# Out-projection weights split beside the values' products, GLA in eight steps a half, and fewer stores of the last q and k

## The chip, the core and the metric

The kernel runs on one core of one Trainium2 chip. A core has five engines with a queue of instructions each: PE (TensorE, matrix products), DVE (VectorE), ACT (ScalarE), POOL (GpSimd) and SP (SyncE, which here issues nearly all transfers). Each works through its own queue in order; semaphores hold an instruction back until what it reads is there and what it overwrites has been read. The metric is the device time of one execution in microseconds (us), as the median of several runs.

## The reference

One layer of a decoder: 1024 tokens of width 1024, normed, go through one input projection; eight heads of differential attention and four heads of gated linear attention (GLA) run in parallel on its columns; the gated results are concatenated and go through one output projection of 2048 x 1024, a norm and the residual. Cut to what matters here:

```
h = rms_norm(x, pre_g)
z = h @ w_in                  # columns: qa ka va ga | qb kb vb gb | gk_low
# differential attention, 8 heads, two maps of 64, values of 128, causal
w  = softmax(q1 k1^T / 8) - lam * softmax(q2 k2^T / 8)
oa = rms_norm(w @ v, subln_g) * 0.8 * silu(ga)
# GLA, 4 heads, keys of 128, values of 256, in chunks of 64
S_t = diag(exp(log_a_t)) S_{t-1} + k_t^T v_t ;  o_t = q_t S_t
ob = rms_norm(o, gla_g) * silu(gb)
y  = concat(oa, ob) @ w_out
out = x + rms_norm(y, post_g)
```

All is float32.

## The kernel before

**Numbers in two parts.** A large product is taken as three products of rounded parts: each operand is split into `hi` (rounded on ACT) and `lo` (the rest, a subtraction on DVE), and hi x hi, lo x hi and hi x lo are summed in a bank of PSUM. So each operand costs a cast on ACT and a subtraction on DVE before PE can use it.

**Input projection.** `w_in` is taken in column blocks with a Strassen scheme: seven products instead of eight for a pair of 2 x 2 blocks. `order` (line 191 on) lists the steps. `("VB", n, kk)` and `("VA", n, kk)` are the wide steps of the GLA and attention values (24 matmuls of 512 columns each); `(p, n)` is product n of narrow pair p of `pairs` (12 matmuls). Each step's weights are split one to a few steps ahead (`prepare`, `block_weights`, `make_weights`). PE's product of n = 1, 6 and 7 goes to bank `x`, 2 and 4 to `y`, 5 and 3 to `z`. `take` and `take_values` finish a unit and store it to DRAM: `k_d`, `q_d` (attention keys and queries, `hi` and `lo`, four stores of 64 rows a unit), `v_d` (attention values), `gq_d`, `gv_d` and so on. Staging tiles of 2 KB a partition come from the tags `st` and `c`, four buffers each.

**Out-projection weights.** Each of the 32 pieces (128 rows x 512 columns, 256 KB) of `w_out` is loaded into `wo_raw` (tag `t4`, one buffer), split, and both parts stored to `wo_d` (`wo_step`, called by `go` behind each narrow step from pair 3 on: a load at n = 1 or 6, a split at n = 1 or 5). Later whole rows come back as `wo_hi`, `wo_lo` (`weights`).

**GLA** runs as a generator (`gla`), advanced by one step behind each narrow product from (8, 5) on, and what is left is run through where eight steps of `order` (`LEAD`) remain. For each head and each half of the tokens: transpose k (`pk`), products within chunks (`pa`), the norm of the half before (`gms`, `gla_norm`), states (`kv`, `gu`), results (two products `gpo`, copied by ACT to `go`), and the sum of squares split into `gqd`, which is the operand of the next `gms`. In `gla` each `yield` ends a step; a half has nine. `gla_norm` stores the finished results to `mixe`.

**Attention.** At the point of the last eight steps, `q`, `k`, `ks` of head 0 are loaded (`load_qk`; `ks` is k with its parts swapped), then weights 8 to 13, the first `mix` tile (token tile 0 of the GLA results, 1 MB in two parts) two steps later, weights 14 and 15. `merge` interleaves three streams by costs: scores (`sc`, minimum on DVE L1131, exponent on ACT L1141, scaling on POOL L1165 and subtraction on DVE L1169 to `p`), values (transposes `wtr`, split to `wt_hi`, `wt_lo`, products `po`) and the out-projection (`out_early`: `ypart`, the GLA half of each token tile as fill for PE, then the attention half, both kept in `y_d`). At the end partial results come back (`yp`) as seeds of the last products `yps`.

**Who sets the order.** The Python code lists instructions; a scheduler then orders each engine's queue by its own estimate of times. `keep_in_program_order` holds an engine's marked instructions in the order of the code (all matmuls, the last stores, the first mix and weight loads), and `issue_after` lets one instruction be issued only behind another. PE, DVE, ACT and SP all execute in the order fixed so.

## Time and profile before

| | |
|---|---|
| median of three runs | 1007.09 us (1006.35 to 1012.83) |
| profiled execution | 1006.61 us, span 1004.9 us |
| PE, DVE, ACT, POOL busy | 964.7, 737.9, 589.9, 144.0 us |
| granted clock of PE, mean | 0.993 |
| moved by DMA | 220.38 MB, mean 219 GB/s |

By the trace: the first scaled transposes of x start at 7.6 us; wide steps, with the first two products of pairs 0 to 2 between them, run until about 191 us; narrow pairs to 628, with GLA beside them from about 350; attention from 630 to about 960; the last products to 998. In stretches of 25 us:

| stretch (us) | PE busy | DVE busy | ACT busy | DMA share |
|---|---|---|---|---|
| 75 to 100 | 25.00 | 15.03 | 4.22 | 0.46 |
| 125 to 150 | 25.00 | 19.52 | 8.18 | 0.37 |
| 175 to 200 | 25.00 | 22.05 | 10.35 | 0.79 |
| 450 to 475 | 25.00 | 19.79 | 14.75 | 0.83 |
| 700 to 725 | 25.00 | 18.31 | 16.29 | 0.59 |

How to read the rows that follow: a row of waits is "engine line waited for: us in total, times, longest"; a row of time is start, duration, engine, line, operation, result<-operands, and in brackets the idle time of the engine before it and who ended it. In a row of a stretch stand its length, busy time with instructions of PE, PE's weight loads, DVE, ACT and POOL, then the granted clock, the DMA share and GB/s. `SPq` is an issue on SP's queue. A DMA row gives how many were issued, KB of each, and the median time from issue to landing.

### The profile page before, as it was taken

The page shows a single profiled execution, that of the slowest core. Times are in us where ns is not written, and L with a number is a line of the kernel's source. Part 1 is how long each engine was busy: PE and PEld are TensorE (multiplying, and loading weights), DVE is VectorE, ACT ScalarE, POOL GpSimd, SP SyncE. Part 2 cuts the span into 40 slices and gives each one's busy share as a digit, 9 for nine tenths or more (in the row PEclk, how much of TensorE's full clock was granted, in tenths as well). Part 3 has the DMA queues.
Part 4 walks back from the last instruction along what each step waited for, and adds up shares of the span by engine and source line. Part 5 has one row for each costly group of instructions (what it writes and reads, how often), then busy time and mean ns, then how long its engine had stood idle before and what let it go on. Part 6 is the DMA issues. An engine that isn't in the chain of part 4 may idle for free.

```text
span 1004.9 us, 14892 instructions
## 1 busy us (share of the span) xinstructions
PE 964.7 (96%) x4866; PEld 809.7 (81%) x4866; DVE 737.9 (73%) x1450; ACT 589.9 (59%) x1152; POOL 144.0 (14%) x153
## 2 busy tenths in 40 slices
PE   6999999999999999999999989799999999999887
PEld 4878888777888888888888877578888888888765
DVE  6996476888899768767787775567777677787545
ACT  8641232445476467755577764357666667777664
POOL 5410000000000000000000000112222233343232
PEclk9999999999999999999999999999999999999999
DMA  9544333755856867788968879896485499875467
GB/s 334 194 123 147 126 105 101 224 147 140 275 184 226 265 214 240 241 282 244 298 220 268 264 271 365 271 335 202 148 270 189 150 320 350 262 202 111 108 204 153
DMA packets 156845, 220.38 MB, mean 219 GB/s; under 512 B 16240, under 2 KB 83824, under 8 KB 156672
## 3 DMA queue, kind: packets, MB, share of 16 engines
q1 hardware_dynamic: 152736, 212.10, 65.4%
q0 software_dynamic: 4032, 7.34, 4.7%
q8 instruction: 38, 0.62, 0.2%
q14 instruction: 39, 0.32, 0.1%
HBM read 133.93 MB, written 88.60 MB: 221 GB/s over the span
## 4 chain that ended last, share of the span: by engine, by line
PE 73%; DMA 9%; DVE 8%; ACT 4%; issue 3%; SPq 1%; POOL 1%; DVEq 0%; ACTq 0%; POOLq 0%
PE x L117 13%; PE v L117 12%; PE ypart L117 11%; PE y L117 8%; PE z L117 8%; PE sc L117 6%; PE po L117 5%; PE yps L117 4%; PE wtr L120 2%; PE gpo L117 2%; DMA w_raw<-in_w_in_dram 2%; DMA k<-k_d 1%; PE kv L117 1%; DMA v_d<-v_hi 1%; DMA wo_d<-wo_raw 1%
## 5 line engine op out<-in xcount | busy, mean ns | idle before, releaser
L1141 ACT ACTIVATE p<-p,stt 128x896 f32<-128x896 f32 (+7 forms) x128 | 99.3, 777 | 47.5 <-DVE stt L1131 40.4
L329 DVE TENSOR_TENSOR w<-w_raw,w 128x512 fp32r<-128x512 f32 x134 | 91.7, 688 | 26.2 <-ACT w L327 26.1
L1131 DVE CUSTOM_DVE_ANT_0 p<-sc,maskt 128x512 f32<-128x512 f32 (+3 forms) x128 | 74.9, 586 | 46.5 <-PE sc L117 45.8
L327 ACT CAST w<-w_raw 128x512 fp32r<-128x512 f32 x134 | 82.7, 619 | 41.2 <-PE y L117 20.2
L1165 POOL TENSOR_SCALAR p<-p,stt,lam 128x1024 f32<-128x1024 f32 (+3 forms) x64 | 61.4, 960 | 204.7 <-DVE stt L1164 190.4
L117 PE MATMUL x<-s_hi,w 128*128 128x512 f32 x320 | 82.0, 399 | 0.0
L117 PE MATMUL z<-s_hi,w 128*128 128x512 f32 x320 | 80.7, 394 | 1.3 <-DVE c L484 1.3
L117 PE MATMUL ypart<-wo_hi,m_hi 128*128 128x512 f32 x192 | 80.5, 419 | 0.1
L117 PE MATMUL y<-h_hi,w 128*128 128x512 f32 x320 | 80.6, 394 | 0.0
L117 PE MATMUL v<-w,s_hi 128*128 128x512 f32 x256 | 79.4, 391 | 0.6 <-DVE w L285 0.5
L117 PE MATMUL ypart<-wo_hi,m_lo 128*128 128x512 f32 x192 | 76.3, 398 | 0.0
L117 PE MATMUL ypart<-wo_lo,m_hi 128*128 128x512 f32 x192 | 76.1, 396 | 0.0
L117 PE MATMUL sc<-k,q 128*128 128x512 f32 (+1 forms) x192 | 71.5, 374 | 2.6 <-DMA ks<-k_d 2.1
L117 PE MATMUL sc<-ks,q 128*128 128x512 f32 (+1 forms) x192 | 67.2, 353 | 4.0 <-DMA ks<-k_d 4.0
L117 PEld LDWEIGHTS x<-s_hi,w 128*128 128x128 f32 x320 | 60.2, 192 | 12.5 <-ACT s L473 0.4
L117 PEld LDWEIGHTS z<-s_hi,w 128*128 128x128 f32 x320 | 59.0, 188 | 13.7 <-DVE c L484 2.2
L117 PEld LDWEIGHTS y<-h_hi,w 128*128 128x128 f32 x320 | 59.0, 188 | 11.6
L256 DVE TENSOR_TENSOR w_raw<-w_raw 128x512 f32<-128x512 f32 x80 | 55.7, 698 | 11.8 <-DMA w_raw<-in_w_in_dram 10.7
L284 ACT CAST w<-w_block 128x1024 fp32r<-128x1024 f32 x24 | 25.1, 1052 | 66.0 <-PE v L117 37.7
L473 ACT COPY s<-x 128x512 f32<-128x512 f32 x60 | 34.9, 581 | 48.4 <-PE x L117 44.0
L1169 DVE SCALAR_TENSOR_TENSOR p<-p,stt,p 128x1024 f32<-128x1024 f32 (+3 forms) x64 | 53.5, 836 | 12.5 <-POOL p L1165 12.2
L892 POOL TENSOR_SCALAR_AFFINE_SELECT gan<-gan 128x512 f32<-128x512 f32 x8 | 5.7, 710 | 390.4 <-ACT gan L891 390.4
(221 smaller groups left out, 2396.2 us busy)
## 6 DMA issues: line engine op xcount, KB each, us to landing
w_raw<-in_w_in_dram SPq DMA_DIRECT2D x40, 512.0 KB, 4.6
w_block<-in_w_in_dram SPq DMA_DIRECT2D x16, 512.0 KB, 4.1
k_d<-qk_st SPq DMA_DIRECT2D x64, 128.0 KB, 2.4
q_d<-qk_st SPq DMA_DIRECT2D x64, 128.0 KB, 3.1
wo_raw<-in_w_out_dram SPq DMA_DIRECT2D x32, 256.0 KB, 3.1
wo_d<-wo_hi SPq DMA_DIRECT2D x32, 256.0 KB, 3.1
wo_d<-wo_raw SPq DMA_DIRECT2D x32, 256.0 KB, 3.5
q<-q_d SPq DMA_DIRECT2D x32, 256.0 KB, 5.4
```

The lines of the kernel that those rows point to most:

```text
L117: tc.keep_in_program_order(pe.matmul(*a, **k))
L120: tc.keep_in_program_order(pe.transpose(dst, src, ident))
L256: dve.tensor_tensor(dst, a, b, ALU.subtract)
L284: act.copy(w[0], src)
L327: act.copy(w[0], src)
L329: split_last[:] = [dve.tensor_tensor(w[1], src, fp(w[0]), ALU.subtract)]
L473: act.copy(b[k], ps)
L892: pool.affine_select(a, a, [[0, 4], [1, P]], ALU.is_ge, 0.0, base=0, channel_multiplier=-1)
L1131: ins = dve.tensor_tensor_reduce(p[:, a:e], sc[:, : e - a], maskt[:, NZ + P - (e - a) :] if last else maskt[:, : e - a], 1.0, 3e38 if i == ...
L1141: act.activation(p[:, :n], p[:, :n], AF.Exp, bias=st[:, m : m + 1], scale=-1.0, accum_out=st[:, 2 + m : 3 + m],)
L1165: pool.tensor_scalar(p1[:, :n], p1[:, :n], st[:, 5:6], lam, ALU.mult, ALU.mult)
L1169: dve.scalar_tensor_tensor(p0[:, :n], p0[:, :n], st[:, 4:5], p1[:, :n], ALU.mult, ALU.subtract)
```

## The change

- **Weights earlier.** A new `wo_wide` is called behind each wide step from ("VB", 5, 0) on: it splits the open piece, in two halves of 256 columns (`wo_hi` from tag `gu`, five buffers), stores the two parts, and loads the next (`wo_load`) while the step after is still ahead of ("VA", 4, 0). That takes 17 of the 32 pieces. The rest go on in narrow steps as before, now also behind n > 2 of pairs 0 to 2.
- **One step in `order`.** For the early pairs product 3 of the pair before stands behind product 6 instead of 5.
- **GLA in eight steps a half.** The step between the second `gpo` and the squares is gone. The buffers of `kq` and `go` change places.
- **Stores of the last q and k.** In the last eight steps all units are staged in one tile of both parts, with two stores of 64 x 2 x 512 each instead of four of 64 x 512.
- **Mix tiles.** Token tiles 0 and 1 are loaded together, in the place where tile 0 was. The rule that tile 1 waits for head 0's values goes.
- **Scores.** From head 1 on, scaling and subtraction of a score block are listed right behind the block, without `issue_after`.
- **End.** The four `yp` loads of the first two token tiles go to two tiles of tag `v` instead of two buffers of `yst`. Costs in `merge` are adapted: the first `ypart` tile counts 0.69 a step instead of 1.

```
@@ order
-            if p and n == (5 if p < EARLY else 2):
+            if p and n == (6 if p < EARLY else 2):
                 order.append((p - 1, 3))
@@ take
-            if ending and order[made[0] - 1][1] == 7:
-                raw = ap.tile([P, 2, 512], F32R, tag="raw", name="qk_st", bufs=4)
-                hi, lo = raw[:, 0], raw[:, 1]
+            both = None
+            if ending and order[made[0] - 1][1] in (7, 3):
+                both = ap.tile([P, 2, 512], F32R, tag="raw", name="qk_st", bufs=4)
+                hi, lo = both[:, 0], both[:, 1]
...
-            for t, src in enumerate((hi, lo)):
-                for m in range(2):
-                    ins = sp.dma_start(d[m, t, :, cs], fp(src)[64 * m : 64 * m + 64])
+            for m in range(2):
+                rows = slice(64 * m, 64 * m + 64)
+                if both is not None:
+                    tc.keep_in_program_order(
+                        sp.dma_start(d[m, :, :, cs].rearrange("t p s -> p t s"), fp(both)[rows])
+                    )
+                    continue
+                for t, src in enumerate((hi, lo)):
+                    ins = sp.dma_start(d[m, t, :, cs], fp(src)[rows])
@@ behind wo_step
+    def wo_wide(more):
+        if wo_open:
+            e, dh, raw = wo_open.pop()
+            lo = raw.bitcast(F32R)
+            for c in range(2):
+                hs = slice(c * 256, c * 256 + 256)
+                hi = ap.tile([P, 256], F32R, tag="gu", name="wo_hi", bufs=5)
+                act.copy(hi, raw[:, hs])
+                dve.tensor_tensor(lo[:, hs], raw[:, hs], fp(hi), ALU.subtract)
+                sp.dma_start(wod[e][0][:, dh * 512 + c * 256 : dh * 512 + c * 256 + 256], fp(hi))
+            sp.dma_start(wod[e][1][:, cols(dh)], fp(lo))
+        if more and wo_todo:
+            wo_load()
@@ go
             if wide(i):
+                if i >= order.index(("VB", 5, 0)):
+                    wo_wide(i + 1 < order.index(("VA", 4, 0)))
                 continue
-            if order[i][0] >= EARLY:
+            if order[i][0] >= EARLY or order[i][1] > 2:
                 wo_step(order[i][1])
@@ gla
-            kq = keys[n] = kp.tile([P, 2, 512], F32, tag="q0", name="kq")
+            kq = keys[n] = kp.tile([P, 2, 512], F32, tag="ks0", name="kq")
-            o = kp.tile([P, 2, 512], F32, tag="ks0", name="go")
+            o = kp.tile([P, 2, 512], F32, tag="q0", name="go")
                 free.append(ib)
-                yield
+                if not m:
+                    yield
@@ the last eight steps
-    mix0 = mix(0)
+    mix0, mix1 = mix(0), mix(1)
@@ scores
+                        while h and scaling:
+                            scale_scores(None)
-            with tc.issue_after(after.ins) if after else nullcontext():
+            with tc.issue_after(after.ins) if after and not h else nullcontext():
@@ out_early
+        nxt = mix1
         for e in range(E, E + 8):
-            yield 1.0
-            if e == E:
-                with tc.issue_after(v_last[0].ins):
-                    nxt = mix(1)
+            yield 0.69
...
+            y2 = smp.tile([P, 2, 512], F32, tag="v", name="yp", bufs=4)
             for dh in range(2):
-                yp = smp.tile([P, 512], F32, tag="yst", name="yp", bufs=2)
-                sp.dma_start(yp, yd[st][dh])
-                seed(st, dh, (Y, SC)[n][dh], yp)
+                sp.dma_start(y2[:, dh], yd[st][dh])
+                seed(st, dh, (Y, SC)[n][dh], y2[:, dh])
```

**SP, at the end of the projections, before.** `mixe` stores are the last GLA results, `m_hi` and `m_lo` the first mix tile, `k_d` the stores of the last keys, `ks` the swapped keys of head 0:

```order
L860 DMA mixe<-gg 128x4x128 x2
L860 DMA mixe<-go 128x4x128 x2
L1021 DMA m_hi<-mixe 128x1024
L1021 DMA m_lo<-mixe 128x1024
L383 DMA k_d<-qk_st 64x512 x8
L974 DMA ks_5607<-k_d 64x512 x4
L974 DMA ks_5612<-k_d 64x512 x4
```

And now, first the place where `ks` and the last `mixe` stores stand:

```order
L886 DMA mixe<-go 128x4x128 x2
L1001 DMA ks_5675<-k_d 64x512
L400 DMA g_d<-g_st 128x512
L1001 DMA ks_5675<-k_d 64x512 x3
L390 DMA q_d<-qk_st 64x512 x4
L998 DMA q_5685<-q_d 128x512 x2
```

then, ten weight loads later, the mix tiles:

```order
L1031 DMA wo_lo<-wo_d 128x1024
L1048 DMA m_hi<-mixe 128x1024
L1048 DMA m_lo<-mixe 128x1024
L1048 DMA m_hi<-mixe 128x1024
L1048 DMA m_lo<-mixe 128x1024
L386 DMA k_d<-qk_st 64x2x512 x4
```

The keys and queries of head 0 have moved from behind the mix tile and the last key stores to ahead of them, the second mix tile has joined the first, and eight key stores have become four.

**SP, in the wide steps of the attention values, before.** `v_d` are stores of values, `wo_raw` the first piece of the out-projection weights:

```order
L654 DMA wo_raw<-in_w_out_dram 128x512
L428 DMA v_d<-v_hi 128x4x128
L428 DMA v_d<-v_st 128x4x128
L428 DMA v_d<-v_hi 128x4x128
L428 DMA v_d<-v_st 128x4x128
L428 DMA v_d<-v_hi 128x4x128 x2
L428 DMA v_d<-v_st 128x4x128 x2
```

Now the same place, from the load of the sixteenth piece on:

```order
L678 DMA wo_raw<-in_w_out_dram 128x512
L670 DMA wo_d<-wo_hi 128x256 x2
L435 DMA v_d<-v_hi 128x4x128 x2
L435 DMA v_d<-v_st 128x4x128 x2
L671 DMA wo_d<-wo_raw 128x512
L678 DMA wo_raw<-in_w_out_dram 128x512
L435 DMA v_d<-v_hi 128x4x128 x2
L435 DMA v_d<-v_st 128x4x128 x2
```

Between the stores of values now stand the stores of a weight piece and the load of the next one, which waits until the store ahead has been read out of the one buffer.

**PE, between the last `gpo` of a GLA half and `gms`, before.** `x`, `y` and `z` are products of the projections:

```order
L117 MATMUL gpo<-gqd,gu 128x128
L117 MATMUL y<-h_hi,w 128x512 x8
L117 MATMUL y<-h_lo,w 128x512 x4
L117 MATMUL x<-s_hi,w 128x512 x8
L117 MATMUL x<-s_lo,w 128x512 x4
L120 MATMUL pk<-ident,kq 128x128 x4
L117 MATMUL x<-h_hi,w 128x512 x8
L117 MATMUL x<-h_lo,w 128x512 x4
L117 MATMUL pa<-kq 128x128 x4
L117 MATMUL y<-h_hi,w 128x512 x8
L117 MATMUL y<-h_lo,w 128x512 x4
L117 MATMUL gms<-gqd,ones 128x512
```

And now:

```order
L117 MATMUL gpo<-gqd,gu 128x128
L117 MATMUL y<-h_hi,w 128x512 x8
L117 MATMUL y<-h_lo,w 128x512 x4
L120 MATMUL pk<-ident,kq 128x128 x4
L117 MATMUL x<-s_hi,w 128x512 x8
L117 MATMUL x<-s_lo,w 128x512 x4
L117 MATMUL pa<-kq 128x128 x4
L117 MATMUL x<-h_hi,w 128x512 x8
L117 MATMUL x<-h_lo,w 128x512 x4
L117 MATMUL gms<-gqd,ones 128x512
```

Four products of the projections stood there, and three stand now. Behind the last half it was two and is three, since GLA ends ahead of the last eight steps: six products more lie between its last `gms` and the first `ypart`. On ACT, 5 to 17 instructions stood from the last copy of `gpo` to the cast into `gqd`, and 5 to 9 now.

17 lines of the change are left out of this document (9 added, 8 removed).

## The prediction

> **What bounds the kernel now.** I read the page's busy times first, then TensorE (PE) alone: the stretches of 25 us, its waits, the order of time around each wait, and last the DMA work there.
>
> ```profile
> PE 964.7 (96%) x4866; PEld 809.7 (81%) x4866; DVE 737.9 (73%) x1450; ACT 589.9 (59%) x1152; POOL 144.0 (14%) x153
> 600.00:625.00 25.00, 20.26 (x82) 16.66 (x83) 12.43 (x19) 10.60 (x18) 0.00 (x0) 0.93 1.02 372
> 625.00:650.00 25.00, 19.80 (x81) 15.26 (x79) 13.90 (x37) 8.82 (x16) 2.28 (x2) 0.93 0.89 276
> 650.00:675.00 25.00, 21.74 (x118) 18.57 (x119) 15.48 (x45) 12.63 (x32) 4.30 (x6) 0.93 0.95 332
> 725.00:750.00 25.00, 25.00 (x152) 22.00 (x151) 19.98 (x57) 17.04 (x42) 8.37 (x8) 1.00 0.69 228
> 925.00:950.00 25.00, 21.84 (x123) 17.66 (x122) 17.46 (x44) 16.34 (x42) 7.49 (x9) 1.00 0.62 152
> PE gms L117 <- DVE gqd L950: 6.2, 2, 5.1
> PE sc L117 <- DMA ks<-k_d: 6.1, 2, 4.0
> PE wtr L120 <- DVE p L1169: 2.9, 2, 1.7
> PE yps L117 <- ACT yps L1462: 1.8, 2, 1.6
> PE z L117 <- DVE c L484: 1.3, 2, 0.7
> ```
>
> PE is busy 964.7 of 1004.9 us, and no edit removes a matmul. So the change can win only from the 40 us in which PE stands still and from stretches at a lower granted clock. A third of the idle time, 5 + 5 + 3 us, lies in one place: the 75 us from the last projections into the first attention head. There the granted clock is 0.93 and the DMA share (next to last column) 0.89 to 1.02. In the middle of attention (725 to 750) PE has no gap.
>
> ```profile
> 604.74 0.79 PE L117 MATMUL gms<-gqd,ones 128*128 128x512 f32 x1 [5.07 <-DVE gqd L950]
> 605.53 6.79 PE x L117 x24
> 236.81 5.44 PE x L117 x24
> 634.66 0.47 PE L117 MATMUL sc<-ks,q 128*128 128x512 f32 x1 [4.04 <-DMA ks<-k_d]
> 635.12 2.15 PE ypart L117 x6
> 637.28 2.19 PE sc L117 x6
> 639.46 1.39 PE ypart L117 x6
> 651.15 0.63 PE L120 MATMUL wtr<-ident,p 128*128 128x128 f32 x4 [1.72 <-DVE p L1169]
> 668.86 0.47 PE L117 MATMUL sc<-k,q 128*128 128x512 f32 x1 [2.07 <-DMA ks<-k_d]
> 670.24 1.28 PE ypart L117 x3
> 672.37 1.05 PE ypart L117 x3
> ```
>
> Each wait costs more than its length: the matmuls behind it run slowly. After the first, 24 take 6.79 us where 24 take 5.44 elsewhere (1.35 lost); after the second, twice six take 2.15 and 2.19 against 1.39 (1.56); after the third, twice three take 1.28 and 1.05 against 1.39 / 2 = 0.69 (0.95). By the Trainium skill, "TensorE: Matmul & The Clock Gate", section "Part 1: The HAM clock gate", PE falls to half rate after an idle window of about 3.4 us and needs some 3.4 us of work to return; that would charge 1.7 us for each of the first two waits and nothing for the third, 3.4 in all where the rows give 3.9. The third wait, 2.07 us, was followed by slow matmuls, so I go by the rows.
>
> **Step 1: the wait for `gms` at the end of GLA (5.07 + 1.35 = 6.4).**
>
> ```profile
> L646 ACT CAST wo_hi<-wo_raw x32: 605/622/634, 249.2 to 601.3; 128x512 fp32r<-128x512 f32 x32
> 499.97 0.59 ACT L939 COPY go<-gpo 128x512 f32<-128x512 f32 x1
> 512.07 0.69 DVE L950 TENSOR_TENSOR gqd<-sq,gqd 64x512 fp32r<-64x512 f32 x1
> 355.45 0.89 PE pa L117 x8
> ```
>
> The last weight piece is cast on ACT at 601.3; ACT and DVE work in order, and behind that cast stand squares and sums of the last GLA half, for which PE waits until 604.74. With no piece left at that time this goes. Eight steps instead of nine also bring `gms` a step nearer to the work before it. In the new order three products of 12 matmuls (5.44 / 2 = 2.72 each) stand between a half's last `gpo` and its `gms`, and `pk` and `pa` (0.89) in all but the last: 8.2 to 9 us. From the copy of `gpo` to the end of `gqd` it took 12.8 us in the slowest half (499.97 to 512.76), with 17 instructions of ACT from copy to cast; there are now 5 to 9, and 12.8 x 9 / 17 is 6.8 us. So 7 us fit, and I book the other wait for `gms` (6.2 - 5.07 = 1.1) as neither won nor lost, and 1 us lost for a half that misses. Bounds: none late, or all eight at 12.8: 8 x 3.8 = 30 us.
>
> **Step 2: `ks` of head 0, and what follows.**
>
> ```profile
> 618.58 3.72 SPq L1021 DMA_DIRECT2D m_hi<-mixe  x1
> 628.15 5.21 SPq L974 DMA_DIRECT2D ks<-k_d  x8
> DMA packets 16135, 30.53 MB, mean 321 GB/s; under 512 B 1872, under 2 KB 5504, under 8 KB 16128
> ```
>
> Before, the `ks` loads go out at 628.15, behind eight small stores and the first mix tile, which itself waits for the last GLA result. In the new order of SP, `q`, `k` and `ks` of head 0 stand ahead of that mix tile and of the last stores, because GLA ends six products (16 us) sooner and frees the buffers. The 4.04 + 1.56 = 5.6 us go. The 1.72 at 651 goes too: between the first scores and the first `wtr` PE has four more groups of three `ypart` matmuls, 4 x 0.69 = 2.8 us.
>
> The third wait (2.07 + 0.95 = 3.0) hangs on DMA. The 95 us from 585 to 680 moved 30.53 MB at 321 GB/s, saturated. By the code's tile sizes the new kernel must land, from the end of the last `s1` product to head 1's first scores, seven weight pairs (7.3 MB), two mix tiles (2.1), six units of q and k (3.1), two heads' values (2.1), head 1's q, k, ks (3.1), gates, a third mix tile and partial results (2.1): 20 MB. At the 372 GB/s of the best stretch that is 53 us, at 350 57. PE has eight products for it (21.8 us), then what lay before between 634.66 and 668.86 without its losses (34.2 - 1.72 - 2.07 - 1.56 = 28.9), the 1.6 before it, and six more `ypart` groups, 4.1: 56 us. With 53 and 57 on its two sides I count half of the 3.0 as won. Twelve stores fewer are no fewer bytes; what SP saves on them is covered by the transfers. Step 2: 5.6 + 1.7 + 1.5 = 8.8.
>
> **Step 3: weights beside the values' products.** Seventeen pieces pass through one buffer: load, two casts, two subtractions, store, and only then the next load. In SP's queue stores of v stand between them, and a wait of SP for a split holds up these; they hold the buffers that DVE needs, and DVE's splits of w stand behind.
>
> ```profile
> 29.48 5.46 PE v L117 x24
> wo_raw<-in_w_out_dram SPq DMA_DIRECT2D x32, 256.0 KB, 3.1
> wo_raw<-in_w_out_dram SPq DMA_DIRECT2D x10, 256.0 KB, 2.8
> wo_d<-wo_raw SPq DMA_DIRECT2D x32, 256.0 KB, 3.5
> wo_d<-wo_raw SPq DMA_DIRECT2D x10, 256.0 KB, 3.0
> L1236 ACT COPY o<-po 128x256 f32<-128x256 f32 x13 | 4.7, 364 | 5.8 <-PE po L117 5.8
> 93.99 0.38 SPq L238 DMA_DIRECT2D w_block<-in_w_in_dram  x1
> 166.74 0.39 SPq L428 DMA_DIRECT2D v_d<-v_hi  x1
> PEld v L117 <- DVE v_st L418: 0.5, 1, 0.5
> ```
>
> A product step of PE is 5.46 us, and each brings one piece. A cycle is the landing of the load (2.8), three operations of 256 columns (0.36 each, by ACT's row) and the landing of the store (3.0): 6.9 us. The landings of 2.8 and 3.0 are those of the ten pieces from 260 to 350; the stretch from 75 to 175 has less traffic, so I take 6.4. The fifth load stands behind the `w_block` that went out at 93.99, and the sixteenth piece's first store ahead of the v store of 166.74. Eleven cycles and 3.9 us to the cast must fit in 72.7: 6.25 us each. Behind that store there is no slack: the next product onto those banks already waits 0.5 us (last row). So each 0.1 us of a cycle above 6.25 costs 1.1: at 6.4 about 2, at 6.9 7. I take 3 us, bounds 0 and 7. By the Trainium skill, "DMA: Bandwidth & Descriptors", section "Anatomy of one DMA", a transfer costs about 2.0 us and its bytes at 436 GB/s (a fit for the GpSimd path), here 2.6; the cycle would be 6.3 and the cost under 1.
>
> In return ACT loses 0.62 us a piece, and DVE about as much, in the stage behind; PE has no other wait there that hangs on them, so nothing more is won. The three early pairs get one more step between the read of a `z` bank and the product onto it: their 1.3 us go.
>
> **Step 4: attention and the end.** The four partial results have own buffers and go out ahead of the last mix tiles: the `yps` waits, 1.8 us, go. From head 1 on, the multiplication on POOL and the subtraction on DVE are issued a score block earlier, so DVE may wait for POOL with one scan between:
>
> ```profile
> L1165 POOL TENSOR_SCALAR p<-p,stt,lam 128x512 f32<-128x512 f32 (+7 forms) x27 | 24.4, 904 | 64.4 <-DVE stt L1164 54.0 <-DMA ks<-k_d 7.1 <-DMA gate<-g_d 3.3
> L1131 DVE CUSTOM_DVE_ANT_0 p<-sc,maskt 128x512 f32<-128x512 f32 (+3 forms) x56 | 32.0, 571 | 16.9 <-PE sc L117 16.7
> ```
>
> That is 0.33 us in each of 56 blocks, 19 us in 250, or 1.9 per 25 on top of DVE's 19.98: below 25, so PE feels little of it. I take 0.5 lost, between 1.1 won (the other `wtr` wait, 2.9 - 1.7) and 19 lost.
>
> **The sum.** Won: 6.4 + 8.8 + 1.3 + 1.8 = 18.3; lost: 1 (late `gms`) + 3 (weights) + 0.5 = 4.5. Net 13.8. The profiled execution took 1006.6 us (span 1004.9 and 1.7 around it), 0.5 under the median of the runs, 1007.1. So 1007.1 - 13.8: about 993 us. If every wait named here went with its slow matmuls (6.4 + 5.6 + 1.7 + 3.0 + 1.3 + 1.8 + 1.1 + 1.1 = 22): 985.
>
> **The rivals.**
> - *The weights set the pace of the values' products, and it gets slower.* With the landings over the whole run (3.1 and 3.5), 1.1 of work, and a wait behind one operation of 0.6 (L646) at each of three places, a cycle is 9.5 us, the v store 11 x 3.25 = 36 us late, and PE with it: 990 + 36 = 1026. It decides from 7.8 us on, where it costs the other 17. For it: one buffer, and SP, ACT and DVE each work in order. Against: few transfers run there beside it. 7 in 100; a milder form, 7 to 7.7 us a cycle, 998 to 1006: 10.
> - *DMA stays the bound of the transition.* At the old mean of 321 GB/s the 20 MB take 62 us, 6 more than PE has: 998; at the 276 of 625 to 650, 72: 1008. For it: three stretches at a share near 1. Against: the lowest rate fell where SP had eight stores of 128 KB and eight such loads to issue. 11.
> - *`gms` is late in most halves*, eight times 1 us or three times 3 and more: 8 to 10 us, 1002. 6.
> - *DVE waits for POOL, and PE with it*: up to 19 us, 1011. 4.
> - *The forecast*, 985 to 998: 58; less than 985: 3.
>
> **Range and chances.** 985 to 1005 leaves out the slow rival, the worst of DMA and POOL, and what is below: some 17 in 100. Faster by over 1% (about what a measurement of this kernel tells from no change) means under 997: nearly all of the forecast, the 3 below it, and a little of the DMA rival, some 60; since most of my small costs are taken high, 0.66. Within 1%: 0.26. Slower by over 1%, over 1017: the slow rival and a rest that I don't see: 0.08.
>
> **What would show it.** Right: no wait of PE for `gms` near the last projections and none over 1 us for `ks` of head 0; PE idle in those 75 us at 2 to 5 us instead of 13, granted clock 0.97 or more; no wait of 1.6 for `yps`. Step 3 right: PE at 24.5 or more in each 25 us from 75 to 200. Wrong: PE waiting for DVE's w in the values' products with ACT waiting for `wo_raw`; `gms` waits in several halves; a `ks` wait at head 1 longer than 3 us.

## The result, and the profile after

The changed kernel is slower: 1016.9 us (median of 12 runs, 1012.1 to 1020.3) against 1006.9 for the kernel before (12 runs, 1004.3 to 1012.8). The ratio is 1.0085, 95% interval 1.0060 to 1.0109. The profiled execution took 1020.3 us, span 1018.6.

The stretches of 25 us of the kernel after, in the values' products with their sum (columns: PE, PEld, DVE, ACT and POOL busy, granted clock, DMA share, GB/s):

```profile
75.00:100.00 25.00, 22.28 (x99) 17.96 (x97) 14.75 (x23) 5.99 (x10) 0.00 (x0) 1.00 0.64 212
100.00:125.00 25.00, 22.40 (x98) 17.94 (x96) 11.55 (x17) 6.27 (x11) 0.00 (x0) 1.00 0.68 216
125.00:150.00 25.00, 22.61 (x88) 17.50 (x89) 13.67 (x19) 7.43 (x14) 0.00 (x0) 0.93 0.44 158
150.00:175.00 25.00, 22.21 (x90) 17.59 (x90) 18.56 (x28) 8.86 (x14) 0.00 (x0) 0.93 0.71 221
175.00:200.00 25.00, 19.02 (x74) 15.23 (x73) 13.73 (x21) 7.88 (x15) 1.69 (x2) 0.86 0.54 172
sum 125.00, PE 108.51 PEld 86.23 DVE 72.27 ACT 36.43 POOL 1.69; mean PE 21.70 PEld 17.25 DVE 14.45 ACT 7.29 POOL 0.34
```

And the same view at the transition:

```profile
625.00:650.00 25.00, 24.05 (x107) 19.57 (x105) 11.26 (x18) 8.03 (x14) 0.00 (x0) 1.00 0.99 366
650.00:675.00 25.00, 23.41 (x102) 19.19 (x103) 14.39 (x41) 10.46 (x20) 3.27 (x3) 0.93 0.91 342
675.00:700.00 25.00, 24.90 (x146) 21.53 (x146) 17.72 (x50) 15.70 (x38) 4.50 (x6) 1.00 0.93 318
```

In the values' products PE had been busy nearly without a gap; now it stands still for 16.5 of 125 us, and the granted clock falls. At the transition it is the other way round: 24.05, 23.41 and 24.90 stand where 20.26, 19.80 and 21.74 stood (from 600 to 675 us, 25 earlier). The waits of PE over the whole run (us in all, times, longest) say the same:

```profile
PE v L117 <- DVE v_st L425: 15.4, 6, 6.0
...
PE x L117 <- ACT s L480: 3.0, 1, 3.0
PE sc L117 <- DMA ks<-k_d: 2.2, 1, 2.2
PE ypart L117 <- DMA m_hi<-mixe: 1.9, 1, 1.9
```

So do those of ACT and DVE from 75 to 215 us:

```profile
ACT wo_hi L668 <- DMA wo_raw<-in_w_out_dram: 63.9, 14, 6.8
DVE wo_raw L669 <- ACT wo_hi L668: 44.7, 13, 6.6
```

The waits for `gms`, for `wtr`'s p and for the `yps` copy are gone; `v_st`, a value tile on its way out, has taken their place with 15.4 us. The stage ends later by more than that, since matmuls behind a wait run slowly: the last product of v starts at 215.54 us, at 190.80 before, 24.7 later. The profiled execution is 13.7 longer than the one before (its span; it is the slowest of the twelve, and the medians differ by 10), so everything behind that stage won about 11 in it. The start of the last product of v, before and after:

```profile
190.80 0.39 PE L117 MATMUL v<-w,h_lo 128*128 128x512 f32 x1
```

```profile
215.54 0.39 PE L117 MATMUL v<-w,h_lo 128*128 128x512 f32 x1
```

SP's queue in order of time shows the pace of the pieces (the fifth and sixth load, the tenth and eleventh, the sixteenth, and the first store of v behind the sixteenth piece):

```profile
101.15 0.33 SPq L678 DMA_DIRECT2D wo_raw<-in_w_out_dram  x1
...
112.10 0.33 SPq L678 DMA_DIRECT2D wo_raw<-in_w_out_dram  x1
...
141.51 0.33 SPq L678 DMA_DIRECT2D wo_raw<-in_w_out_dram  x1
...
147.72 0.33 SPq L678 DMA_DIRECT2D wo_raw<-in_w_out_dram  x1
...
184.81 0.33 SPq L678 DMA_DIRECT2D wo_raw<-in_w_out_dram  x1
...
189.97 1.04 SPq L435 DMA_DIRECT2D v_d<-v_hi  x2
```

The chain of waits ahead of PE's longest stall (start, us, what):

```profile
178.68 2.65 DMA wo_raw<-in_w_out_dram
...
182.72 2.07 DMA wo_d<-wo_raw
184.81 3.78 DMA wo_raw<-in_w_out_dram
...
189.00 0.40 ACT wo_hi L668
189.40 1.05 ACT v_hi L432 x2
190.47 2.54 DMA v_d<-v_hi
...
193.44 0.69 DVE v_st L425
...
194.17 2.08 PE v L117 x4
```

Eleven cycles take 83.66 us, 7.6 each, but they are not alike: five of them take 6.0 to 6.2 (such as the one from 141.51), and in these SP issues no store of v and no `w_block` load; the six with such transfers between take 6.6 to 11.0 (such as the one from 101.15). The store of v that went out at 166.74 before goes at 189.97; `v_hi` waits on ACT behind a weight's cast, that cast for the load, the load for the landing of the store before it. Which link of that does the harm, the rows alone don't say.

### The profile page after: what moved, and what is told of

The parts are those of the page before. It is cut to its first block, busy times and chain, and to the rows that moved or that the text cites. A ratio compares the mean times of both kernels' runs of the same rounds, so it can differ in the third digit from the quotient of the medians.

```text
span 1018.6 us, 14888 instructions
## 1 busy us (share of the span) xinstructions
PE 973.4 (96%) x4866; PEld 814.5 (80%) x4866; DVE 740.4 (73%) x1467; ACT 594.6 (58%) x1169; POOL 141.2 (14%) x153
## 4 chain that ended last, share of the span: by engine, by line
PE 64%; DMA 12%; DVE 4%; ACT 3%; issue 3%; SPq 1%; POOL 0%; DVEq 0%; ACTq 0%; POOLq 0%
PE x L117 14%; PE z L117 9%; PE ypart L117 9%; PE y L117 8%; PE sc L117 5%; PE po L117 4%; PE yps L117 4%; PE gpo L117 3%; PE v L117 2%; DMA wo_raw<-in_w_out_dram 2%; PE wtr L120 2%; DMA wo_lo<-wo_d 1%; DMA ks<-k_d 1%; DMA q_d<-qk_st 1%; DMA wo_d<-wo_raw 1%
## 5 line engine op out<-in xcount | busy, mean ns | idle before, releaser
L117 PE MATMUL v<-w,s_hi 128*128 128x512 f32 x256 | 83.3, 406 | 14.1 <-DVE v_st L425 12.9
L1193 POOL TENSOR_SCALAR p<-p,stt,lam 128x1024 f32<-128x1024 f32 (+3 forms) x64 | 55.3, 866 | 228.6 <-DVE stt L1192 218.5
L117 PEld LDWEIGHTS x<-s_hi,w 128*128 128x128 f32 x320 | 60.0, 191 | 15.4 <-ACT s L480 3.5
L117 PEld LDWEIGHTS v<-w,s_hi 128*128 128x128 f32 x256 | 49.5, 196 | 28.1 <-DVE v_st L425 15.6
L117 PE MATMUL v<-w,h_hi 128*128 128x512 f32 x192 | 61.9, 410 | 3.2 <-DVE v_st L425 2.5
L117 PEld LDWEIGHTS po<-wt_hi,v 128*128 128x128 f32 x320 | 54.6, 190 | 7.3 <-ACT wt_hi L1235 1.0
L117 PE MATMUL po<-wt_hi,v 128*128 128x256 f32 (+1 forms) x320 | 59.6, 277 | 0.6 <-ACT wt_hi L1235 0.6
```

The source lines that it names most:

```text
L117: tc.keep_in_program_order(pe.matmul(*a, **k))
L1193: pool.tensor_scalar(p1[:, :n], p1[:, :n], st[:, 5:6], lam, ALU.mult, ALU.mult)
```

## The experiments

All times are set against the kernel before, run beside them on the same chip (its medians there 1008.9 to 1010.9), so ratios are compared rather than medians from different groups. "Last v" is the start of the last product of v, by the order of time; `v_st` the wait of PE for it.

| kernel | median, us | ratio to before, 95% | last v | `v_st` |
|---|---|---|---|---|
| before | 1006.9 | | 190.80 | 0 |
| after | 1016.9 | 1.0085 (1.0060 to 1.0109) | 215.54 | 15.4 |
| no_wide | 1004.4 | 0.9948 (0.9923 to 0.9973) | 190.24 | 0 |
| wide_alone | 1027.6 | 1.0176 (1.0129 to 1.0223) | 213.65 | 13.6 |
| dma_pool | 1027.3 | 1.0187 (1.0138 to 1.0235) | 198.33 | 4.8 |
| split_pool | 1031.0 | 1.0206 (1.0159 to 1.0252) | 207.43 | 11.6 |
| lo_out | 1012.8 | 1.0017 (0.9987 to 1.0047) | 210.69 | 10.8 |
| half_pace | 1008.8 | 0.9981 (0.9957 to 1.0006) | 202.26 | 8.1 |
| two_raw | 1012.2 | 1.0023 (1.0000 to 1.0045) | 209.12 | 8.9 |
| two_raw_late | 1009.8 | 0.9983 (0.9961 to 1.0006) | 210.61 | 9.4 |
| no_split | 1019.8 | 1.0082 (1.0050 to 1.0114) | 215.98 | 19.1 |
| two_nosplit | 1012.0 | 1.0024 (0.9998 to 1.0051) | 208.86 | 1.2 |
| half_pool | 1002.2 | 0.9910 (0.9882 to 0.9939) | 195.10 | 2.4 |
| all_pool | 1055.7 | 1.0449 (1.0386 to 1.0511) | 191.74 | 0.7 |
| two_pool | 991.6 | 0.9822 (0.9779 to 0.9864) | 192.65 | 0.8 |
| lo_nine | 1018.2 | 1.0068 (1.0038 to 1.0097) | 206.67 | 9.9 |
| lo_unmerged | 1017.8 | 1.0054 (1.0021 to 1.0088) | 209.56 | 11.8 |
| two_pool_again | 992.1 | 0.9815 (0.9791 to 0.9840) | 191.30 | 0 |
| old_scores | 988.9 | 0.9782 (0.9750 to 0.9814) | 191.29 | 0 |
| one_mix | 995.2 | 0.9854 (0.9824 to 0.9883) | 192.56 | 0 |

### Where the loss lies: no_wide and wide_alone

`no_wide` takes the pieces beside the values' products out of the new kernel; `wide_alone` puts only them into the old one.

```diff
             if wide(i):
-                if i >= order.index(("VB", 5, 0)):
-                    wo_wide(i + 1 < order.index(("VA", 4, 0)))
                 continue
```

> The new kernel without the weight pieces beside the values' products: all 32 pieces are split in the narrow product steps again, now from the first pair on. Theory (the loss lies in the values' products alone): the last product of v ends near 191 us, as before, and not at 215.6; no wait of PE for v_st; the time is 1016.9 - 24.7, and up to 5 less if the wait at 282 us goes too: 987 to 992. Rival (the end of GLA is quiet only because 17 pieces are done by then): a wait of PE for gms of 5 us and its slow matmuls come back there, 994 to 1000. Second rival (the new stores, loads or order cost something of their own): above 1000.

> The kernel before with only the weight pieces beside the values' products added. Theory (the loss lies there and hangs on no other edit): last product of v near 215 us, 24.7 lost; the wait for gms at the end of GLA goes, 6.4 won: 1006.9 + 18 = 1025, with 1019 to 1031 as bounds. Rival (the loss comes from the weights together with another of the edits): the last product of v before 200 us, 1001 to 1010.

The stage behaves as the theory said in both: last v at 190.24 without the pieces, at 213.65 with them alone, and the time of `wide_alone`, 1027.6, lies in its bounds. But `no_wide` won only 4.5 us, where 15 to 20 were expected. The waits of PE in `no_wide`:

```profile
PE gms L117 <- DVE gqd L975: 7.4, 3, 5.1
...
PE x L117 <- ACT s L480: 2.7, 1, 2.7
```

The rival was half right: the waits for `gms` are back, the longest in the middle of GLA and not at its end. The time itself, 1004.4, lies where the second rival had it, above 1000; these two waits, 10.1 us without their slow matmuls, stand against the 12 to 17 that it missed by. In the kernel after, the last piece is cast at 385.6 us and no half waits; in `no_wide` the casts go on until 576.0, and three halves wait, until 442, 473 and 507 us, the last the longest (none later, though pieces are still split there). So it helps to have the pieces done early, and what had to be found is how to do them there without the loss.

### Which queue: dma_pool and split_pool

`dma_pool` lets POOL issue the pieces' loads and stores, `split_pool` lets POOL do their casts and subtractions.

```diff
-                sp.dma_start(wod[e][0][:, dh * 512 + c * 256 : dh * 512 + c * 256 + 256], fp(hi))
-            sp.dma_start(wod[e][1][:, cols(dh)], fp(lo))
+                pool.dma_start(wod[e][0][:, dh * 512 + c * 256 : dh * 512 + c * 256 + 256], fp(hi))
+            pool.dma_start(wod[e][1][:, cols(dh)], fp(lo))
...
-        sp.dma_start(raw, w_out[0, e * P : (e + 1) * P, cols(dh)])
+        (q or sp).dma_start(raw, w_out[0, e * P : (e + 1) * P, cols(dh)])
```

```diff
-                act.copy(hi, raw[:, hs])
-                dve.tensor_tensor(lo[:, hs], raw[:, hs], fp(hi), ALU.subtract)
+                pool.tensor_copy(hi, raw[:, hs])
+                pool.tensor_tensor(lo[:, hs], raw[:, hs], fp(hi), ALU.subtract)
```

> The new kernel with the loads and stores of the weight pieces beside the values' products issued by POOL, which has nothing to do there; the splits stay on ACT and DVE. If the harm is that the stores of v stand behind waiting weight transfers in SP's queue: PE waits under 5 us in the values' products, last product of v before 198 us, 995 to 999. If the harm is that ACT and DVE stand behind a wo_raw that has not landed: ACT waits for wo_raw some 60 us as now, PE loses 15 to 25 us, 1008 to 1018. If both in equal parts: 1003 to 1008.

> The new kernel with the casts and subtractions of the weight pieces beside the values' products done by POOL; loads and stores stay in SP's queue. If the harm is that ACT and DVE stand behind a wo_raw that has not landed: PE waits under 5 us there, 994 to 999. If the harm is SP's queue, where v's stores stand behind waits for the split: PE loses as much as now or more, since POOL's operations are longer (0.9 us for 512 columns and more), 1014 to 1030. If both in equal parts: 1003 to 1010.

Taking the transfers out of SP's queue brought last v from 215.54 to 198.33; taking the work off ACT and DVE only to 207.43. As to the time both failed, for a reason that no expectation had named: the pieces themselves now ran late on POOL's side, and the low-rank weights (`wd`), whose tile lies in the same one buffer, could be loaded only when the last piece had been stored out of it. PE's wait in `dma_pool`, and in order of time the store of the last piece and the load behind it:

```profile
PE gkl_ps L117 <- DVE wl L740: 26.1, 1, 26.1
...
224.63 0.54 POOL L671 DMA_DIRECT2D wo_d<-wo_raw  x1
...
227.02 0.37 SPq L735 DMA_DIRECT2D wd<-in_w_in_dram  x1
```

PE stands still for 26.1 us before the low-rank products (`gkl_ps`), for 21.3 in `split_pool`. Without that wait `dma_pool` would be at about 1001 (an estimate, 1027.3 less 26.1). So one buffer is too slow for a piece a step even with nobody else in the queue: POOL's sixteen cycles from 69.39 to 220.03 us take 9.4 each, where a step takes 5.46.

### The buffer, the rate, the splits: lo_out, half_pace, two_raw, no_split

`lo_out` writes the low part to a tile of its own, so that the next load need not wait for a store. `half_pace` does a piece only beside every second product. `two_raw` has two buffers and splits a piece one step after its load. `no_split` leaves the splits out and stores raw bytes. Their edits in this order:

```diff
-            lo = raw.bitcast(F32R)
+                lo = ap.tile([P, 256], F32R, tag="gu", name="wo_lo", bufs=5)
```

```diff
-                if i >= order.index(("VB", 5, 0)):
-                    wo_wide(i + 1 < order.index(("VA", 4, 0)))
+                i0, i1 = order.index(("VB", 5, 0)), order.index(("VA", 4, 0))
+                if i >= i0 and (i - i0) % 2 == 0:
+                    wo_wide(i + 2 < i1)
```

```diff
+        if more and wo_todo:
...
+            if wide_n[0] % 2:
+                raw = ap.tile([P, 512], F32, tag="t4", name="wo_raw", bufs=1)
+                raw = [raw[:, :256], raw[:, 256:]]
+            else:
+                raw = [ap.tile([P, 256], F32, tag=f"gu{c}", name="wo_raw", bufs=1) for c in range(2)]
...
+        if wide_open and (len(wide_open) > 1 or not more):
+            e, dh, raw = wide_open.pop(0)
```

```diff
-                act.copy(hi, raw[:, hs])
-                dve.tensor_tensor(lo[:, hs], raw[:, hs], fp(hi), ALU.subtract)
-                sp.dma_start(wod[e][0][:, dh * 512 + c * 256 : dh * 512 + c * 256 + 256], fp(hi))
+                sp.dma_start(wod[e][0][:, dh * 512 + c * 256 : dh * 512 + c * 256 + 256], raw[:, hs])
-            sp.dma_start(wod[e][1][:, cols(dh)], fp(lo))
+            sp.dma_start(wod[e][1][:, cols(dh)], raw)
```

> The new kernel, but the low part of each weight piece beside the values' products is written to a tile of its own and stored from there in two halves, so that the one wo_raw buffer is free after the subtractions and not after the landing of the store. Bytes and work are the same, one DMA issue a piece more. Theory (the pace is set by the round trip through that buffer): a cycle loses the store's landing of 2.3 us, 7.6 becomes 5.3, under the 5.46 of a product step; last product of v before 195 us instead of 215.6, PE at 24.5 or more in each 25 us from 75 to 200; 993 to 998. Rival (it is the weights' traffic, with v's stores and the w_block loads slower under it, or the casts' own time on ACT and DVE): the last product of v stays after 207 us, 1008 to 1018.

> The new kernel with a weight piece beside every second product step of the values only, 8 pieces instead of 17; the other nine go to the narrow steps. Theory (a cycle of 6 to 7.6 us must fit between two pieces, and has 10.9 now): no wait for v_st, last product of v before 195 us; the last piece is split near 480 us, inside GLA, so a wait for gms of 1 to 3 us may be back in its middle, none at its end: 992 to 998. Rival (any piece there delays v's stores, whatever the pace): half of the loss stays, last product of v near 203 us, 1004 to 1008.

> The new kernel with two buffers for the weight pieces beside the values' products, in the same space: a piece is loaded in one step and split in the next, while the following one is on its way. Pieces, bytes and work on ACT and DVE are the same. The runs so far leave two theories. One (ACT and DVE stand in order behind a load that SP issued just ahead, some 3 to 4 us a piece, and the work on v behind them is late): ACT waits for wo_raw under 15 us in the values' products instead of 64, PE for v_st under 3, last product of v before 196 us, 993 to 999. The other (the pieces' traffic or their work on ACT and DVE is what delays v): last product of v after 203 us, 1004 to 1012.

> The new kernel with the splits beside the values' products left out: each piece is loaded into the one buffer and its raw bytes are stored to both places, so loads, stores and their order in SP's queue stay, and ACT and DVE have nothing to do with them (the weights' low parts are wrong for these 17 pieces). If ACT and DVE standing behind the loads is the harm: no wait for v_st over 1 us, last product of v before 195 us, 991 to 997. If SP's queue and the traffic are the harm: the last product of v stays after 203 us, 1004 to 1015.

My theory fell in all four. With the store off the round trip (`lo_out`) last v came back by 4.9 us, with two buffers by 6.4, with half of the pieces by 13.3. The loss per piece hardly depends on the rate: 24.7 / 17 = 1.5 us at a piece a step, 11.5 / 8 = 1.4 at a piece every second step; PE's first three waits for `v_st` in `half_pace` (2.8, 1.2 and 2.4 us) are those of the kernel after (2.7, 1.2 and 2.5). And with no work on ACT and DVE at all the loss was as large as in the new kernel. The waits of DVE in `no_split` from 75 to 215 us, and of SP's queue, where L666 stores a piece and L674 loads the next:

```profile
DVE v_st L425 <- issue: 20.0, 2, 13.8
DVE v_st L425 <- DMA gv_d<-v_st: 9.2, 5, 3.7
...
SPq L666 <- DMA wo_raw<-in_w_out_dram: 35.9, 16, 3.6
SPq L674 <- DMA wo_d<-wo_raw: 32.4, 18, 4.0
```

And the stall of PE, in its order of time:

```profile
152.94 1.22 PE L117 MATMUL v<-w,s_hi 128*128 128x512 f32 x2 [12.76 <-DVE v_st L425]
```

DVE has the product and cannot write it: the `v_st` tiles are still full, because SP, which must store them, stands at a weight's transfer whose bytes or buffer are not ready, 68 us in all.

### Both queues at once: two_pool, all_pool, half_pool, two_nosplit

`two_pool` is `two_raw` without pieces in the first three pairs of the narrow steps, and with the pieces' transfers issued by POOL. `all_pool` has transfers and splits on POOL, one buffer. `half_pool` is `half_pace` with POOL's queue, also without the early pieces. `two_nosplit` is `two_raw` on SP's queue without splits. `two_pool` against `two_raw`:

```diff
-                sp.dma_start(raw[c], w_out[0, e * P : (e + 1) * P, c0 : c0 + 256])
+                pool.dma_start(raw[c], w_out[0, e * P : (e + 1) * P, c0 : c0 + 256])
...
-                    sp.dma_start(wod[e][t][:, hs], fp(src))
+                    pool.dma_start(wod[e][t][:, hs], fp(src))
...
-            if order[i][0] >= EARLY or order[i][1] > 2:
+            if order[i][0] >= EARLY:
```

The other three put together lines shown above.

> As two_raw_late (two buffers, split one step after the load, early pairs without pieces), with the weights' loads and stores beside the values' products issued by POOL. Theory of two queues (SP held by waits for buffers or casts, and ACT and DVE held by loads, each enough by itself to delay v; so that neither change alone helped): last product of v before 195 us, no wait for v_st over 1.5 us, no wait for wl behind POOL over 3 us; 990 to 995. Theory of traffic (v's stores and the loads of w land later beside the weights, whoever issues them): last product of v after 200 us, 1000 to 1010.

> The new kernel with one buffer, a piece beside every second product step, loads and stores issued by POOL, and no pieces in the first three pairs. POOL's round trip (9.4 us in the run with all pieces) fits into two steps of 5.46. Theory of two queues: only ACT and DVE are held, 8 times; half of what dma_pool lost (8 us) stays: last product of v at 194 to 197, no backlog on POOL; with waits for gms of 2 to 3 us in GLA 993 to 999. Theory of traffic: last product of v after 198 us.

> The new kernel with all that the weight pieces beside the values' products need on POOL: loads, casts, subtractions, stores, through the one buffer. Only the traffic is left beside the work on v. Theory of two queues: the last product of v is before 194 us, as before the change; POOL itself falls behind (its round trip is longer than a step), and the low-rank weights wait for it 20 us and more: 1010 to 1035. Theory of traffic: the last product of v is after 200 us.

> As two_raw, with the splits beside the values' products left out: raw bytes are loaded and stored to both places, one step later, from two buffers (the weights' low parts are wrong for these pieces). ACT and DVE have no part in it, and SP waits neither for a cast nor for the store of the step before. Theory of two queues (in no_split SP's round trip of load, store and next load through one buffer, 5.6 us and more, was longer than a step): last product of v before 195 us, 990 to 997. Theory of traffic: after 203 us, 1004 to 1015.

`two_pool` beats both kernels: 991.6 us, 0.9822 of before; run again beside the last two experiments 992.1, 0.9815 (0.9791 to 0.9840). Its stretches in the values' products:

```profile
125.00:150.00 25.00, 25.00 (x111) 20.45 (x110) 20.53 (x28) 10.64 (x18) 10.07 (x20) 1.00 0.62 195
...
175.00:200.00 25.00, 24.89 (x110) 19.83 (x109) 23.15 (x41) 9.82 (x17) 2.13 (x6) 1.00 0.91 263
```

ACT waits for a piece 23.2 us from 75 to 215 us instead of 63.9, and PE 0.8 for `v_st`.

Four kernels with 17 pieces, one a step, give a table of two by two, in starts of the last v:

| | SP issues | POOL issues |
|---|---|---|
| one buffer | 215.5 (after) | 198.3 (dma_pool) |
| two buffers | 210.6 (two_raw_late) | 192.7 (two_pool) |

SP's queue costs 17 to 18 us in either row, the one buffer 5 to 6 in either column, and 1.9 are left against 190.8. So the two add; that each was enough by itself, as the expectation had it, is wrong. The cells are not quite alike: by its last v, `dma_pool` had loaded 14 of its 17 pieces and the others all 17, and with two buffers one or two pieces are loaded before 69 us. Traffic is innocent but for at most those 1.9: `two_pool` moves 28.1 MB from 75 us to its last v, 239 GB/s, where the kernel after moves 28.4 at 202; its stores of v and loads of w land later still, and PE stands still for 1.0 us. (`all_pool`, whose last v starts at 191.74, says less about this: it had loaded only 11 pieces by then.) Landings of stores of v and of loads of w from 75 to 200 us in the kernel after (KB each, median us; in the kernel before they took 2.6 and 3.7):

```profile
w_block<-in_w_in_dram SPq DMA_DIRECT2D x7, 512.0 KB, 4.4
gv_d<-v_st SPq DMA_DIRECT2D x12, 256.0 KB, 4.1
```

And in `two_pool`:

```profile
w_block<-in_w_in_dram SPq DMA_DIRECT2D x7, 512.0 KB, 5.0
gv_d<-v_st SPq DMA_DIRECT2D x12, 256.0 KB, 4.8
```

As a time `all_pool` is the worst, and beyond the 1010 to 1035 expected: its pieces are so late on POOL that PE waits 56.8 us for the low-rank weights. `half_pool` is at 195.10 as expected, but its total, 1002.2, is not: with 24 pieces left for the narrow steps the waits for `gms` came to 7.3 us, not 2 to 3. `half_pace` has the same 24, but begins them in the first three pairs and casts the last at 488.6 us, where `half_pool` casts it at 518.6; its waits for `gms` are 2.5. `two_nosplit` ended late, as the theory of traffic had it, for another reason. Order of time on SP and DVE:

```profile
144.57 0.38 SPq L743 DMA_DIRECT2D wd<-in_w_in_dram  x1
...
147.38 0.23 DVE L745 TENSOR_TENSOR wd<-wd 128x64 f32<-128x64 f32 x1 [16.31 <-DMA wd<-in_w_in_dram]
```

PE gets its next weights 10.2 us late from that.

The low-rank weights (`wd`) stand behind the pieces in SP's queue, and DVE, which has them early in its order there, behind `wd`. Again a queue, not the bytes; but this run alone could not have told it from traffic.

### The other terms: two_raw_late, lo_nine, lo_unmerged, old_scores, one_mix

```diff
-            if order[i][0] >= EARLY or order[i][1] > 2:
+            if order[i][0] >= EARLY:
```

> As two_raw, but in the narrow steps the pieces begin with the fourth pair, as before the change, and not in the first three. If those early pieces cause the wait of PE for ACT's s near 282 us, of 3 us with as much again in slow matmuls: it goes, and the time is 3 to 6 us below two_raw. If the wait comes from the loads of w there: the same time.

The ratio falls from 1.0023 to 0.9983, 4 us (2.4 by the medians), and PE's wait for ACT's `s` is gone. The early pieces were its cause. (The intervals of the two ratios still meet, so the 4 us are rough.)

`lo_nine` has the `yield` of the second `go` copy back, `lo_unmerged` the old stores of q and k, both on top of `lo_out`:

```diff
-                if not m:
-                    yield
+                yield
```

```diff
-            if ending and order[made[0] - 1][1] in (7, 3):
+            if ending and order[made[0] - 1][1] == 7:
...
-                if both is not None:
+                if False:
```

> As lo_out, with GLA in nine steps a half as before the change. If the eight steps carry the gain at the transition (the buffers of q, k and ks come free 16 us earlier): the wait for ks of head 0 is back with 3 to 5 us and its slow matmuls, 5 to 8 us slower than lo_out. If it is the weights that are out of the way by then which carry it: 0 to 2 us slower than lo_out.

> As lo_out, with the last stores of q and k issued as before the change: eight more stores of 128 KB, half of the last units through the four small buffers. If SP's issues are covered by the transfers, as the prediction had it: the same time as lo_out within 1.5 us. If the number of stores delays the loads of head 0: a wait for ks of 2 to 5 us, 3 to 7 us slower than lo_out.

Both are 5 us slower than `lo_out` by the medians (4 to 5 by the ratios, whose intervals still meet), though their last v is not later (206.67 and 209.56 against 210.69). From the first to the last partial product it takes 300.1 us in `lo_out`, 304.8 and 304.2 in these (its row in `lo_unmerged`: count, least, median and most ns, first and last start):

```profile
L117 PE MATMUL ypart<-wo_hi,m_lo x192: 387/394/796, 645.3 to 949.5; 128*128 128x512 f32 x192
```

So the eight steps and the fewer stores each carry about 5 us of the gain; in `lo_unmerged` twelve stores more are issued, not the eight of its expectation. What is late in both is a wait that I had not named: `po`, the products of head 0's or 1's scores with v, for ACT's `wt_hi`. PE's order of time in `lo_nine`:

```profile
678.47 0.80 PE L117 MATMUL po<-wt_hi,v 128*128 128x256 f32 x2 [2.58 <-ACT wt_hi L1234]
```

It is 1.85 us in `lo_unmerged` and 0.35 in `lo_out`, and the granted clock of the stretch from 675 to 700 is 0.86 and 0.93 there, 1.00 in `lo_out`. In `lo_nine` 3.3 us of `gms` waits are back too. The wait for `ks` of head 0 that I had expected in both is in neither.

`old_scores` and `one_mix` undo one edit each in `two_pool`.

```diff
-                        while h and scaling:
-                            scale_scores(None)
```

```diff
-    mix0, mix1 = mix(0), mix(1)
+    mix0 = mix(0)
```

> The kernel of two_pool once more, beside the two that follow, for an interval and for the comparison with them: 990 to 994, 0.978 to 0.987 of the kernel before.

> As two_pool, with the scaling and subtraction of the scores of heads 1 to 7 issued where they stood before the change, a score block later. The prediction took 0.5 us lost for the new place, bounds 1.1 won and 19 lost: if it is right, within 1.5 us of two_pool, and the wait of PE's wtr for p of about 1.7 us is back. If DVE waits for POOL in the new place, this one is faster by 2 us or more.

> As two_pool, with the second mix tile loaded where it was before the change, behind the values of head 0. If the second tile ahead of them crowds the transfers of the transition: the wait of ypart for m_hi (2.4 us) or of sc for ks (2.2) gets shorter, 1 to 3 us faster than two_pool. If the transition is bound by its bytes whatever their order: the same within 1.5 us. If the tile is needed early: a new wait for it at the second row of partial products, 1 to 4 us slower.

`old_scores` is the quickest of all: 988.9 us (988.0 to 989.4) against 992.1 (989.8 to 994.0) in `two_pool_again`. Its four runs all lie below the six of the other, though the intervals of the two ratios still meet. From the first to the last partial product it takes 299.5 us in `two_pool_again`:

```profile
L117 PE MATMUL ypart<-wo_hi,m_lo x192: 386/394/671, 621.3 to 920.8; 128*128 128x512 f32 x192
```

and 296.7 in `old_scores`:

```profile
L117 PE MATMUL ypart<-wo_hi,m_lo x192: 387/394/796, 622.1 to 918.8; 128*128 128x512 f32 x192
```

The first has two waits in its order of time that the second lacks, but for 0.3 us of the second:

```profile
849.01 0.47 PE L117 MATMUL sc<-k,q 128*128 128x512 f32 x1 [1.59 <-DVE p L1211]
852.32 0.47 PE L117 MATMUL sc<-ks,q 128*128 128x512 f32 x1 [1.24 <-DMA ks<-k_d]
```

Which of them costs the 3 us is open: the profiled execution of `two_pool`, the same kernel, has no wait for p and 2.2 us for `ks`. The cause that the expectation named is not seen: from 640 to 930 us DVE waits for POOL 6.5 us in `two_pool_again` and 7.7 in `old_scores`. Nor is the wait of `wtr` for p back with 1.7 us there; it is 0.5. `one_mix` is 3 us slower than `two_pool_again`, with a new wait for the second mix tile (in PE's order of time):

```profile
642.98 0.47 PE L117 MATMUL ypart<-wo_hi,m_hi 128*128 128x512 f32 x1 [2.41 <-DMA m_hi<-mixe]
```

Its third case came true: the tile ahead is needed early.

## Why the prediction was wrong

Forecast were 993 us, faster at 0.66. Point by point:

- **Step 3, the weights beside the values' products, is the step that failed.** It was the term of 3 us (bounds 0 and 7), and the stage lost 24.7. The path was named: a wait of SP holds up v's stores, and these hold the buffers that DVE needs; that is the chain shown above. Its price was wrong. First, the size of the cycle: 6.4 us came from landings and work alone, and 7.6 was measured. The bare round trip was even a little better than forecast (6.0 to 6.2); the rest lies in the cycles that have v's stores or the loads of w between them in the same queue, 6.6 to 11.0 each. By the step's own rule, 1.1 us for each 0.1 above 6.25, 7.6 is 15 us, and the time 993 + 12 = 1005. The rival "the weights set the pace" had the same mechanism (one buffer; SP, ACT and DVE each in order) and 10 in 100 in its milder form, with 998 to 1006. Second, the form of the price. I compared the cycle with the step, as if below 6.25 nothing were lost. `half_pace` shows a loss per piece of the same size with a piece every 10.9 us: each time SP stands at a transfer that is not ready, v's stores behind it wait at once. By the Trainium skill, "DMA: Bandwidth & Descriptors", section "Anatomy of one DMA", load and store of 256 KB would be 2.6 us each (an estimate by its fit); they landed in 3.2 and 2.3 from 75 to 240 us, 5.5 together against 5.2, so the transfers nearly agree. What was not in that sum is the waiting between them: 7.6 less 5.5 and 1.1 of work, 1.0 a cycle on average.
- **Within step 3 a cost was overlooked.** The pieces in the first three pairs were booked only as "one more step", which won 1.3 (the `z` waits are 0.2 now, so that held). The pieces themselves cost 2 to 4 us there, by `two_raw_late`; that term stood at nothing.
- **Step 1** (6.4 less 1): right in size, half right in cause. No wait for `gms` is left in the kernel after. `no_wide` and `half_pool` have the eight steps and 7.4 and 7.3 us of waits, none of them at the end of GLA; `lo_nine` has the early weights and 3.3, of which 2.5 at the end of GLA. Both edits are needed for none at all.
- **Step 2** (8.8): right as to what goes. `ks` of head 0 and `wtr` do not wait, and PE is idle 2.6 us at the first partial product (1.9 and 0.7, for a mix tile) where three waits stood: within the 2 to 5 us that were named as the sign, with the granted clock of the three stretches at 0.98 on average. "Twelve stores fewer are covered by the transfers" was wrong: `lo_unmerged` puts them at about 5 us.
- **Step 4**: the `yps` copy's 1.8 went as said. The scores' 0.5 is nearer to 3, within the bounds (1.1 won to 19 lost); why is open.
- **The sum.** Taken out of the wrong term it holds: won were to be 18.3, less 1 and 0.5. `two_pool` keeps every other edit but the early pieces and loses 1.9 in the stage; run again, it was 18.7 us faster than before (1010.9 and 992.1). That it comes out so closely is partly luck: the scores cost some 2.5 us more than booked, so the other terms won as much more.

The range reached to 1005, where the milder rival lay with its cycle of 7 to 7.7 us. The cycle came out there; what a cycle costs was too small, 15 us instead of 24.7, and the early pieces, up to 4 us, were missing: 1005 + 9.7 + 4 = 1019, against 1016.9 measured.

## What to carry to other kernels

A background load, split and store in a queue that also carries the stage's own stores costs each time the queue's head waits, not only when its round trip is longer than a step: price it by the wait of the queue per piece. Give such work a queue that has nothing else to do, and two buffers, so that the consumer comes a step after the load; here the first was worth 17 to 18 us, the second 5 to 6, and with a piece a step only both together beat the kernel before. And look at what else shares the buffer: a small tile that had to wait for the last piece kept PE standing for 26 us.

## What the hardware showed unexpectedly

POOL as issuer. By the Trainium skill, "DMA: Bandwidth & Descriptors", section "Issuing engines are not separate DMA queues", transfers issued by different engines run on the same 16 DMA engines, so issuing from several saves only the time of issuing. The landings agree, even a little against POOL; in `dma_pool` from 75 to 240 us:

```profile
wo_d<-wo_raw POOLq DMA_DIRECT2D x17, 256.0 KB, 2.8
...
wo_raw<-in_w_out_dram POOLq DMA_DIRECT2D x16, 256.0 KB, 3.3
```

and in the kernel after, in the same stretch:

```profile
wo_raw<-in_w_out_dram SPq DMA_DIRECT2D x17, 256.0 KB, 3.2
...
wo_d<-wo_raw SPq DMA_DIRECT2D x16, 256.0 KB, 2.3
```

The time does not: `two_raw_late` and `two_pool` differ in the issuer alone, by 18 us of last v and 16 to 18 of the whole (by the ratios and by the medians). What is saved is not the issuing (0.33 us a load on SP) but the waits that stand ahead of each issue in an engine's order.

The other point is the clock. The 16.5 us in which PE stands still in the values' products cost 24.7, half as much again: up to its last v PE is also busy 8.4 us longer (124.1 against 115.7, from 75 us on), since the granted clock of the stretches from 125 on is 0.93 to 0.86 where it was 1.00. The longest of these waits is 6.0 us, and the three next ones 2.5 to 2.7. So a wait well under 3 us is enough to lower the clock here: after the one of 2.5 us that ended at 126.11 it is 0.70 from 126 to 130 us, and in the kernel before, after the one of 2.07 us that ended at 668.86, it is 0.50 from 671 to 673.
